# Rotation and norm of queries and keys in a dilated attention: from GpSimd and VectorE to VectorE alone

## The chip, the cores and the metric

One NeuronCore of a Trainium2 chip runs the whole program. The metric is the device time of one execution in microseconds (us). Before the change the median of three runs is 1305.77 us (1304.62 to 1307.18).

## The reference, cut to what matters

A decoder trunk of two layers works on one sequence of 256 tokens with 1024 channels in float32. Each layer is SwiGLU, attention, SwiGLU. The attention of layer 0 is a mixture of three dilations; the change is in how its queries and keys are made.

```python
def dilated_mixer(u, w_qkv, q_gain, k_gain, w_o):
    qkv = (u @ w_qkv).reshape(b, s, N_DIL, 3, N_HEADS, HEAD_DIM)      # 3 dilations, q k v, 16 heads of 64
    for g in range(N_DIL):
        q = rope(rms_norm(qkv[:, :, g, 0], q_gain[g]))
        k = rope(rms_norm(qkv[:, :, g, 1], k_gain[g]))
        o, lse = dilated_attention(q, k, qkv[:, :, g, 2], DIL_WINDOWS[g], DIL_RATES[g])
...
    w = jax.nn.softmax(jnp.stack(lses, axis=0), axis=0)               # merge of the dilations
```

The attention of layer 1 (`nsa_mixer`) is sparse: compressed blocks, selected blocks and a window, with two shared key heads. The change touches the order in which its units may end.

## The kernel before, in words

Every product is made of three matmuls on a high and a low part of each operand. A weight block arrives by DMA as 128x2048 float32 in a ring of four (`st`). Each half of it (128x1024) is cast on ScalarE to the high part (`wh`, line 387) and subtracted on VectorE to the low part (`wl`, line 413); both rings hold six halves. Between the weights stand blocks of `w_ada`, which VectorE reduces (line 393). All blocks come in one fixed order.

The dilated attention works through four head groups of four heads. For each of them `dilated` (line 1062) makes three projections of queries and keys, one for each dilation (`project`, 48 matmuls of 512 columns on lines 849 to 851, with four halves of weights), then two projections of values. A projection uses its first two halves in matmuls 1 to 24 and its last two in 25 to 48. Each projection of queries and keys is followed by a task, `qk_task` (line 919). There are twelve of these tasks. One task does, for both tiles of 128 tokens: squares on ScalarE (860); rotation, which is three multiplications on VectorE (890, 894) and an addition (895); sums of squares (864); an inverse root by a seed (877, 879) and three Newton steps (`newton`, lines 577 to 590); a multiplication of the rotated values with the result (938); and eight transposes on TensorE (906), whose copies go to ScalarE (912). Before the change the additions, the Newton steps and the last multiplications are on GpSimd, for VectorE the Newton step has three instructions instead of four.

Then come the units (`dil_unit`), four in a head group: scores on TensorE (967, 969), mask and maximum on VectorE (975), exponentials on ScalarE (983), division on VectorE (989, 991), transposes (906), copies on ScalarE and VectorE (914), and the product with the values (1007), which after the second unit of a head pair is split into two parts (275, 276).

The order of the instructions on each engine is fixed when the program is built, and each engine works through its queue in that order. A planner, `_Clock`, decides it with a model of each engine's time: a task says with `clk.V(n)`, `clk.G(n)` and `clk.on(...)` how long its parts take, and yields the time at which its next part is to be issued; `fill` issues weight splits and `w_ada` reductions while the modelled VectorE is not too far ahead. So a number in `qk_task` sets behind how many matmuls the task's transposes stand in TensorE's queue, and which splits stand ahead of a task and which behind it in VectorE's.

In the sparse attention a unit (`nsa_unit`, line 1436) is one head pair and one tile of queries. Two units share one half of a PSUM bank (`opair`), and before the change the unit of the second tile copies it out.

Of the kernel before, what the change touches and what calls it, by code (L numbers as in the profile page):

```python
# [72 lines left out]
TT = 2  # L73
# [150 lines left out]
class _Kernel:  # L224
# [194 lines left out]
    def fill(self):  # L419

        clk = self.clk
        while not self.hold:
            T = clk.now + self.slack
            if self.lows and self.lows[0][0][2] < clk.now + self.lag and clk.free["V"] < T:
                self.low()
# [6 lines left out]
            e = self.queue[self.qpos][0]  # L432
            if self.staged[self.qpos][1] > T:
                return
            if e[0] == "w":
                if len(self.halves) >= self.released + self.depth or clk.free["A"] > T:
                    return
            elif clk.free["V"] > T:
                return
# [134 lines left out]
                if len(self.halves) < self.released + self.depth and self.queue[self.qpos][0][0] == "w":  # L574
                    self.emit()

    def newton(self, eng, x, y, n):

        nc = self.nc
        t = self.small(n, f"rs_t{n}")  # L580
        eng.tensor_tensor(out=t, in0=y, in1=y, op=ALU.mult)  # L581
        z = self.small(n, f"rs_y{n}")
        if eng is nc.gpsimd:
            eng.tensor_tensor(out=t, in0=t, in1=x, op=ALU.mult)  # L584
            eng.tensor_scalar(out=t, in0=t, scalar1=-0.5, scalar2=1.5, op0=ALU.mult, op1=ALU.add)  # L585
            eng.tensor_tensor(out=z, in0=t, in1=y, op=ALU.mult)  # L586
        else:
            eng.scalar_tensor_tensor(out=t, in0=t, scalar=-0.5, in1=x, op0=ALU.mult, op1=ALU.mult)
            eng.scalar_tensor_tensor(out=z, in0=t, scalar=1.5, in1=y, op0=ALU.add, op1=ALU.mult)
        return z  # L590
# [8 lines left out]
    def modulated(self, gs, sh, timed=False):  # L599
# [22 lines left out]
        self.hold = False  # L622
        T = self.clk.on("V", 800 * KC, self.clk.now)
        self.clk.free["A"] = max(self.clk.free["A"], T)
# [243 lines left out]
        return self.head_newton(x, self.head_seed(x, n), n, eng)  # L868

    def head_newton(self, x, y, n, eng=None):  # L870
        for _ in range(3):
            y = self.newton(eng or self.nc.gpsimd, x, y, n)
        return y

    def head_seed(self, x, n):
# [43 lines left out]
    def qk_task(self, ps, q, k, g):  # L919

        nc = self.nc
        x = self.small(16, "qkx")
        R = []
        clk = self.clk
        sq = [self.head_squares(ps[tt], 8) for tt in range(TT)]
        for tt in range(TT):
            clk.A(512, clk.now)
            T = clk.G(512, clk.V(1280, clk.now))
            R.append(self.rope(ps[tt].rearrange("p (a r d) -> p a r d", r=4, d=HD),
                               self.dtab[g][:, 0, tt], self.dtab[g][:, 1, tt]).rearrange("p a r d -> p (a r) d"))  # L930
        for tt in range(TT):
            self.head_sums(x[:, tt * 8:(tt + 1) * 8], sq[tt])
            T = clk.V(512)
        rs = self.head_rstd(x, 16)
        T = clk.on("G", 1700, clk.on("V", 400, T))
        for tt in range(TT):
            T = clk.G(512)
            nc.gpsimd.tensor_tensor(out=R[tt], in0=R[tt],  # L938
                                    in1=rs[:, tt * 8:(tt + 1) * 8].unsqueeze(2).to_broadcast([P, 8, HD]),
                                    op=ALU.mult)  # L940
        yield T
        for tt in range(TT):
            c = slice(tt * P, (tt + 1) * P)
            self.transpose4((q[:, :, c], k[:, :, c]), R[tt].rearrange("p h d -> p (h d)"))
# [491 lines left out]
    def nsa_unit(self, kv, pr, qt, oh, ol):  # L1436
        nc, clk = self.nc, self.clk
# [3 lines left out]
        n = (qt + 1) * P  # L1441
# [50 lines left out]
        half = len(pts) // 2  # L1492
        o = self.opair(pr)
        steps = [(b, tt) for b in range(2) for tt in range(qt + 1)]
        while not self.done[kv]:
            yield clk.now + 500.0
        yield "P", 265.0 * (len(steps) + 1), {}, {"u": 1}
        for e in range(2):
            r = slice(e * 64, e * 64 + 64)
            mm(out=o[r, qc], lhsT=self.vpr[kv][:, pr, r], rhs=self.pcT[kv][:, qc], start=True, stop=False)  # L1500
        for i, (b, tt) in enumerate(steps):
            for e in range(2):
                vc = (b * 2 + kv) * HD
                mm(out=o[e * 64:e * 64 + 64, qc], lhsT=self.vkv[:, tt, vc:vc + HD], rhs=pts[e * half + i],
                   start=False, stop=i == len(steps) - 1)
        if qt == 1:
            yield "A", 270.0
            j = kv * 4 + pr
            nc.scalar.copy(out=oh[j], in_=o)
            yield "V", 340.0  # L1510
            nc.vector.tensor_tensor(out=ol[j], in0=o, in1=oh[j].bitcast(F32), op=ALU.subtract)
            self.odone.add(j)

    def nsa_mixer(self, u, gate_fn, prep):
        clk = self.clk
# [1 line left out]
        halves = self.filler  # L1517
        self.warm(AF.Exp)
        self.slack = SL
        self.nsa = {}  # L1520

        self.normed, self.ready, self.done = [False, False], [0, 0], [False, False]
        self.taken, self.blocks = [False, False], False
# [31 lines left out]
        p = self.tmp((P, 2, S))  # L1555
# [304 lines left out]
```

## Time and profile before

| | before |
|---|---|
| median of three runs | 1305.77 us |
| profiled execution, its own time | 1304.5 us |
| its span | 1302.7 us |
| TensorE busy | 1224.2 us, 94% |
| VectorE busy | 976.3 us, 75% |
| GpSimd busy | 255.3 us, 20% |

The span runs from the first to the last instruction; 1.8 us of the profiled execution lie outside it. The dilated attention fills 232 to 560 us of the span. A busy share is a mean over stages; what an engine waited for is read in its own stage.

### The profile page before, as it was taken

To read this page: it belongs to the slowest core of one execution; us is meant where nothing else is said; L and a number is where in the kernel's file an instruction comes from. 1 tells how busy PE (TensorE), PEld (TensorE's weight loads), DVE (VectorE), ACT (ScalarE), POOL (GpSimd) and SP (SyncE) were. 2 spreads that over 40 slices of the span, in tenths; PEclk is the share of its full clock that TensorE was granted. 3 is DMA by queue.
4 is the path that set the end of the run, shared out by engine and by line. 5 is a ranking of instruction groups with operands and counts; after the bars stand their busy time and mean duration, and the time that the engine had idled before them with its cause. 6 is when DMAs were issued, how large, how long until landed. Compare 5 with 4: busy or idle time off the path is not lost.

```text
span 1302.7 us, 23375 instructions
## 1 busy us (share of the span) xinstructions
PE 1224.2 (94%) x9373; PEld 1146.2 (88%) x9373; DVE 976.3 (75%) x1743; ACT 646.3 (50%) x1126; POOL 255.3 (20%) x356
## 2 busy tenths in 40 slices
PE   4899999789989898899999999999999889999998
PEld 3899999677777687799999999989998778999998
DVE  6788886866768677578888878878778997766652
ACT  4545554434445444456545446545435477654441
POOL 3460010462433525110000100030001353000000
PEclk9999999989999999899999999999999899999999
DMA  8889877534353544245888956776983003466650
GB/s 324 303 300 341 325 302 280 196 148 173 133 203 148 197 134 163 91 163 206 327 321 320 343 208 242 272 276 244 334 311 142 33 2 132 162 257 227 239 198 17
DMA packets 42733, 284.50 MB, mean 218 GB/s; under 512 B 5249, under 2 KB 6273, under 8 KB 9346
## 3 DMA queue, kind: packets, MB, share of 16 engines
q1 hardware_dynamic: 42626, 283.02, 58.8%
q8 instruction: 73, 1.20, 0.4%
q14 instruction: 34, 0.28, 0.1%
HBM read 281.96 MB, written 1.05 MB: 217 GB/s over the span
## 4 chain that ended last, share of the span: by engine, by line
PE 73%; DVE 13%; POOL 8%; ACT 3%; issue 2%; DMA 0%; SPq 0%; ACTq 0%; DVEq 0%; POOLq 0%
PE mm L466 18%; PE mm L467 18%; PE mm L468 18%; PE mm L849 3%; PE mm L850 3%; PE mm L851 3%; DVE wl L413 2%; PE tp L906 2%; POOL y L938 2%; POOL rs_t L581 2%; POOL rs_t L584 2%; POOL rs_y L586 2%; POOL rs_t L585 1%; DVE y L1455 1%; DVE st L393 1%
## 5 line engine op out<-in xcount | busy, mean ns | idle before, releaser
L413 DVE TENSOR_TENSOR wl<-st,wh 128x1024 fp32r<-128x1024 f32 x361 | 436.3, 1234 | 94.4 <-ACT wh L387 94.0
L387 ACT CAST wh<-st 128x1024 fp32r<-128x1024 f32 x361 | 369.4, 1048 | 137.3 <-PE mm L468 45.3
L466 PE MATMUL mm<-uh,wh 128*128 128x256 f32 x1304 | 366.5, 281 | 1.6 <-DVE y L738 1.6
L467 PE MATMUL mm<-uh,wl 128*128 128x256 f32 x1304 | 367.9, 282 | 0.0
L468 PE MATMUL mm<-ul,wh 128*128 128x256 f32 x1304 | 365.0, 280 | 0.0
L468 PEld LDWEIGHTS mm<-ul,wh 128*128 128x128 f32 x1304 | 246.8, 189 | 0.0
L466 PEld LDWEIGHTS mm<-uh,wh 128*128 128x128 f32 x1304 | 244.5, 187 | 1.9 <-DVE y L738 1.8
L467 PEld LDWEIGHTS mm<-uh,wl 128*128 128x128 f32 x1304 | 245.0, 188 | 0.0
L466 PE MATMUL mm<-y,wh 128*128 128x256 f32 x832 | 233.4, 281 | 0.1
L467 PE MATMUL mm<-y,wl 128*128 128x256 f32 x832 | 232.4, 279 | 0.0
L468 PE MATMUL mm<-y,wh 128*128 128x256 f32 x832 | 232.2, 279 | 0.0
L393 DVE CUSTOM_DVE_ANT_0 st<-st,cact 128x1024 f32<-128x1024 f32 x152 | 186.7, 1258 | 0.0
L466 PEld LDWEIGHTS mm<-y,wh 128*128 128x128 f32 x832 | 156.4, 188 | 1.1 <-issue 0.9
L467 PEld LDWEIGHTS mm<-y,wl 128*128 128x128 f32 x832 | 156.4, 188 | 0.0
L468 PEld LDWEIGHTS mm<-y,wh 128*128 128x128 f32 x832 | 156.4, 188 | 0.0
L849 PE MATMUL mm<-wh,uh 128*128 128x512 f32 (+1 forms) x336 | 135.0, 402 | 0.0
L850 PE MATMUL mm<-wl,uh 128*128 128x512 f32 (+1 forms) x336 | 131.0, 390 | 0.1
L851 PE MATMUL mm<-wh,ul 128*128 128x512 f32 (+1 forms) x336 | 130.3, 388 | 0.0
L524 POOL TENSOR_TENSOR y<-y 128x256 f32<-128x256 f32 x20 | 22.8, 1138 | 360.3 <-ACT y L505 360.3
L895 POOL TENSOR_TENSOR y<-y 128x512 f32<-128x512 f32 (+1 forms) x26 | 32.3, 1251 | 265.4 <-DVE y L894 157.5
L737 ACT ACTIVATE y<-mm 128x256 f32<-128x256 f32 x84 | 32.2, 383 | 94.2 <-PE mm L468 94.0
L849 PEld LDWEIGHTS mm<-wh,uh 128*128 128x128 f32 x336 | 66.3, 197 | 14.1 <-issue 1.2
(254 smaller groups left out, 1659.2 us busy)
## 6 DMA issues: line engine op xcount, KB each, us to landing
st<-w_in SPq DMA_DIRECT2D x88, 1024.0 KB, 5.1
st<-w_ada SPq DMA_DIRECT2D x76, 1024.0 KB, 5.7
st<-w_out SPq DMA_DIRECT2D x44, 1024.0 KB, 6.8
st<-w_qk SPq DMA_DIRECT2D x24, 1024.0 KB, 4.8
st<-w_va SPq DMA_DIRECT2D x8, 1024.0 KB, 4.7
st<-w_o SPq DMA_DIRECT2D x8, 1024.0 KB, 4.8
st<-w_vb SPq DMA_DIRECT2D x4, 1024.0 KB, 5.0
st<-w_q SPq DMA_DIRECT2D x4, 1024.0 KB, 6.8
```

What stands on the lines that cost most here:

```text
L387: nc.scalar.copy(out=wh, in_=src)
L393: nc.vector.tensor_tensor_reduce(out=src, in0=src, in1=self.cact, scale=1.0, scalar=0.0, op0=ALU.mult, op1=ALU.add, accum_out=self.mod[:, ...
L413: (self.nc.gpsimd if eng == "G" else self.nc.vector).tensor_tensor(out=o, in0=src[:, c], in1=i.bitcast(F32), op=ALU.subtract)
L466: mm(out=out, lhsT=ah, rhs=bh, start=start, stop=False, **kw)
L467: mm(out=out, lhsT=al, rhs=bh, start=False, stop=False, **kw)
L468: mm(out=out, lhsT=ah, rhs=bl, start=False, stop=stop, **kw)
L581: eng.tensor_tensor(out=t, in0=y, in1=y, op=ALU.mult)
L737: nc.scalar.activation(out=sg, in_=ps[:, 0:S], func=AF.Silu)
L849: mm(out=ps[tt], lhsT=uh[k][:, c], rhs=wh[:, o], start=k == 0, stop=False)
L850: mm(out=ps[tt], lhsT=uh[k][:, c], rhs=wl[:, o], start=False, stop=False)
L851: mm(out=ps[tt], lhsT=ul[k][:, c], rhs=wh[:, o], start=False, stop=k == KC - 1)
L895: (eng or nc.gpsimd).tensor_tensor(out=A, in0=A, in1=B, op=ALU.add)
```

## The change

The addition of the rotation, the Newton steps and the last multiplication of `qk_task` go to VectorE, and so do their modelled times. The last Newton step of a task writes a tile with a ring of its own (`rs16`). In the sparse attention the unit that ends second, whichever it is, copies the pair out, and a unit waits until the pair before it in the same half bank has been copied.

```diff
     def head_newton(self, x, y, n, eng=None):
-        for _ in range(3):
-            y = self.newton(eng or self.nc.gpsimd, x, y, n)
+        for i in range(3):
+            y = self.newton(eng or self.nc.gpsimd, x, y, n, "rs16" if n == 16 and i == 2 else None)
...
         for tt in range(TT):
             clk.A(512, clk.now)
-            T = clk.G(512, clk.V(1280, clk.now))
             R.append(self.rope(ps[tt].rearrange("p (a r d) -> p a r d", r=4, d=HD),
-                               self.dtab[g][:, 0, tt], self.dtab[g][:, 1, tt]).rearrange("p a r d -> p (a r) d"))
+                               self.dtab[g][:, 0, tt], self.dtab[g][:, 1, tt], nc.vector)
+                     .rearrange("p a r d -> p (a r) d"))
+            T = clk.V(1880, clk.now)
...
-        rs = self.head_rstd(x, 16)
-        T = clk.on("G", 1700, clk.on("V", 400, T))
+        rs = self.head_rstd(x, 16, nc.vector)
+        T = clk.on("V", 2300, T)
         for tt in range(TT):
-            T = clk.G(512)
-            nc.gpsimd.tensor_tensor(out=R[tt], in0=R[tt],
+            T = clk.V(512)
+            nc.vector.tensor_tensor(out=R[tt], in0=R[tt],
...
-        while not self.done[kv]:
-            yield clk.now + 500.0
+        j = kv * 4 + pr
+        while not self.done[kv] or j > 1 and j - 2 not in self.odone:
+            yield clk.now + 300.0
...
-        if qt == 1:
+        self.half_done[j] = self.half_done.get(j, 0) + 1
+        if self.half_done[j] == TT:
             yield "A", 270.0
-            j = kv * 4 + pr
             nc.scalar.copy(out=oh[j], in_=o)
```

VectorE's queue, first head group, before: from the seed of the first task to the start of the second (`wl<-st,wh` is a weight split, `mod<-` a reduction of `w_ada`, `y<-mm` the rotation).

```order
L879 TENSOR_SCALAR rs_y_2859<-qkx 128x16
L413 TENSOR_TENSOR wl<-st,wh 128x1024 x4
L393 ISA st,mod<-st,cact 128x1024
L393 ISA mod 128x1
L393 ISA st,mod<-st,cact 128x1024
L393 ISA mod 128x1
L413 TENSOR_TENSOR wl<-st,wh 128x1024 x2
L890 TENSOR_TENSOR y<-mm,shareA 128x512
```

The same place after, from the first Newton step's end to the splits.

```order
L589 SCALAR_TENSOR_TENSOR rs_y_2863<-rs_t_2861,rs_y_2859 128x16
L581 TENSOR_TENSOR rs_t_2866<-rs_y_2863 128x16
L588 SCALAR_TENSOR_TENSOR rs_t_2866<-rs_t_2866,qkx 128x16
L589 SCALAR_TENSOR_TENSOR rs_y_2868<-rs_t_2866,rs_y_2863 128x16
L581 TENSOR_TENSOR rs_t_2871<-rs_y_2868 128x16
L588 SCALAR_TENSOR_TENSOR rs_t_2871<-rs_t_2871,qkx 128x16
L589 SCALAR_TENSOR_TENSOR rs_2873<-rs_t_2871,rs_y_2868 128x16
L939 TENSOR_TENSOR y<-y,rs_2873 128x512 x2
L413 TENSOR_TENSOR wl<-st,wh 128x1024 x3
```

Nine Newton instructions and two multiplications now stand between a task's seed and the next split; before, the split came next. The first split behind the task is in both the third half of the second projection.

VectorE's queue, first head group, before: from the end of the second task to the start of the third (`y<-mm,shareC`).

```order
L879 TENSOR_SCALAR rs_y_2997<-qkx 128x16
L413 TENSOR_TENSOR wl<-st,wh 128x1024 x2
L393 ISA st,mod<-st,cact 128x1024
L393 ISA mod 128x1
L393 ISA st,mod<-st,cact 128x1024
L393 ISA mod 128x1
L413 TENSOR_TENSOR wl<-st,wh 128x1024 x2
L890 TENSOR_TENSOR y<-mm,shareC 128x512
```

The same place after.

```order
L939 TENSOR_TENSOR y<-y,rs_3008 128x512 x2
L413 TENSOR_TENSOR wl<-st,wh 128x1024 x2
L393 ISA st,mod<-st,cact 128x1024
L393 ISA mod 128x1
L890 TENSOR_TENSOR y<-mm,shareC 128x512
```

Before, all four halves of the projection that runs beside the third task (the values) were split ahead of it. Now two are, and the third and fourth come behind the whole third task.

VectorE's queue, second head group, after: from the end of the fifth task (`rs_3559`) on, with a unit's split, a unit's division and the next unit's mask ahead of the next weight splits.

```order
L939 TENSOR_TENSOR y<-y,rs_3559 128x512 x2
L276 TENSOR_TENSOR y<-o,y 128x256
L990 RECIPROCAL rd<-den 128x2
L992 TENSOR_SCALAR y<-y,rd 128x512 x2
L976 ISA y,mx<-sc,shareB 128x512
L976 ISA mx 128x1
L976 ISA y,mx<-sc,shareB 128x512
L976 ISA mx 128x1
L981 TENSOR_SCALAR nb<-mx 128x2
L413 TENSOR_TENSOR wl<-st,wh 128x1024 x2
```

The same place before, behind the fifth task's seed.

```order
L879 TENSOR_SCALAR rs_y_3621<-qkx 128x16
L989 RECIPROCAL rd<-den 128x2
L991 TENSOR_SCALAR y<-y,rd 128x512 x2
L413 TENSOR_TENSOR wl<-st,wh 128x1024
L914 COPY y<-tp 128x512
L413 TENSOR_TENSOR wl<-st,wh 128x1024
```

Here too the third half of a projection (the third one of the head group) now stands behind a whole task, and behind a unit's work as well. On GpSimd all 192 instructions of the twelve tasks are gone; VectorE has 156 more.

## Rows read from the trace of the kernel before

**Rows 1.** The page's first part: busy time, share of the span and number of instructions of each engine.

```profile
PE 1224.2 (94%) x9373; PEld 1146.2 (88%) x9373; DVE 976.3 (75%) x1743; ACT 646.3 (50%) x1126; POOL 255.3 (20%) x356
```

**Rows 2.** Busy time in stretches of the span: from the start to the end, length, busy us of PE, PEld, DVE, ACT, POOL (with instructions), granted clock of TensorE (1.00 is 2.4 GHz, 0.50 is 1.2 GHz), share of the DMA engines, GB/s. The dilated attention, the end of the SwiGLU stage before it, and the SwiGLU stage after it.

```profile
220.00:240.00 20.00, 20.00 (x140) 18.50 (x139) 15.33 (x35) 9.78 (x19) 0.00 (x0) 1.00 0.31 110
240.00:560.00 320.00, 283.27 (x1601) 229.48 (x1600) 219.60 (x397) 141.42 (x256) 134.98 (x192) 0.94 0.44 163
...
600.00:820.00 220.00, 220.00 (x1862) 219.93 (x1862) 183.77 (x280) 115.08 (x170) 6.13 (x5) 1.00 0.78 288
```

**Rows 3.** The longest wait of TensorE in the whole span: who waited for whom, us in total, times, longest.

```profile
PE tp L906 <- POOL y L938: 34.6, 14, 7.6
```

**Rows 4.** The dilated attention in order of time, at its first task: start us, us, engine, line, operation, and in brackets the idle time before and what ended it.

```profile
244.08 0.40 PE L849 MATMUL mm<-wh,uh 128*128 128x512 f32 x1
244.31 0.40 PE L850 MATMUL mm<-wl,uh 128*128 128x512 f32 x1
...
244.61 0.69 DVE L890 TENSOR_TENSOR y<-mm,shareA 128x512 f32<-128x512 f32 x1 [1.67 <-ACT y L860]
...
245.88 0.68 DVE L890 TENSOR_TENSOR y<-mm,shareA 128x512 f32<-128x512 f32 x1
...
248.74 0.18 DVE L879 TENSOR_SCALAR rs_y<-qkx 128x16 int32<-128x16 int32 x1
248.82 4.66 DVE L413 TENSOR_TENSOR wl<-st,wh 128x1024 fp32r<-128x1024 f32 x4
...
250.10 0.19 PEld L850 LDWEIGHTS mm<-wl,uh 128*128 128x128 f32 x1 [0.48 <-DVE wl L413]
...
250.19 1.08 POOL L584 TENSOR_TENSOR rs_t<-rs_t,qkx 128x16 f32<-128x16 f32 x1
...
258.53 0.22 POOL L584 TENSOR_TENSOR rs_t<-rs_t,qkx 128x16 f32<-128x16 f32 x1
...
260.53 1.69 PE L906 MATMUL tp<-ident,y 128*128 128x128 f32 x6 [7.60 <-POOL y L938]
```

**Rows 5.** Stretches of 10 us around pauses of TensorE, columns as in rows 2.

```profile
250.00:260.00 10.00, 2.88 (x12) 1.99 (x11) 8.08 (x10) 0.90 (x1) 9.02 (x13) 0.75 0.78 302
260.00:270.00 10.00, 9.47 (x36) 7.67 (x37) 4.01 (x9) 4.28 (x8) 3.95 (x4) 0.74 0.31 117
...
440.00:450.00 10.00, 6.36 (x30) 4.88 (x29) 5.08 (x7) 1.74 (x4) 8.15 (x13) 0.97 0.81 312
450.00:460.00 10.00, 10.00 (x67) 9.10 (x66) 4.12 (x4) 5.48 (x11) 0.00 (x0) 0.85 0.31 107
```

**Rows 6.** In order of time, VectorE in the sparse attention: a whole rotation on VectorE, the sums, two multiplications by the inverse root, and small instructions each of which needs the one before.

```profile
1027.11 1.27 DVE L864 TENSOR_REDUCE qkx<-y 128x8 f32<-128x512 f32 x2
1028.41 0.18 DVE L877 TENSOR_SCALAR qkx<-qkx 128x16 f32<-128x16 f32 x1
1028.62 0.17 DVE L879 TENSOR_SCALAR rs_y<-qkx 128x16 int32<-128x16 int32 x1
1028.70 0.68 DVE L890 TENSOR_TENSOR y<-mm,qtab 128x512 f32<-128x512 f32 x1
...
1030.74 0.68 DVE L890 TENSOR_TENSOR y<-mm,qtab 128x512 f32<-128x512 f32 x1
...
1033.21 0.69 DVE L1329 TENSOR_TENSOR y<-mm,rs_y 128x512 f32<-128x512 f32 x1 [0.40 <-POOL rs_y L586]
1033.82 0.68 DVE L1360 COPY y<-tp 128x512 f32<-128x512 f32 x1
...
1041.99 0.25 DVE L1424 RECIPROCAL cden<-cden 128x16 f32<-128x16 f32 x1
1042.28 0.17 DVE L1426 TENSOR_TENSOR cden<-cden,gts 128x16 f32<-128x16 f32 x1
```

**Rows 7.** In order of time, VectorE's Newton step of the row norm before the stage.

```profile
228.35 0.16 DVE L581 TENSOR_TENSOR rs_t<-rs_y 128x2 f32<-128x2 f32 x1
228.55 0.16 DVE L588 SCALAR_TENSOR_TENSOR rs_t<-rs_t,rs_x 128x2 f32<-128x2 f32 x1
228.74 0.16 DVE L589 SCALAR_TENSOR_TENSOR rs_y<-rs_t,rs_y 128x2 f32<-128x2 f32 x1
```

**Rows 8.** The same columns for the four stretches of the stage: from the first projection's start to the mask of the first unit of the first head group (line 975), from there to the first mask of the second head group's units, to that of the third's, and from there to the split after the last unit (line 276). The units of a head group run beside the projections of the next one.

```profile
232.40:303.29 70.89, 56.48 (x236) 43.90 (x235) 46.34 (x79) 29.47 (x49) 38.87 (x48) 0.88 0.51 193
303.29:381.97 78.68, 71.73 (x410) 58.43 (x409) 55.52 (x100) 36.56 (x65) 32.21 (x48) 0.96 0.44 159
381.97:459.47 77.50, 70.32 (x410) 57.33 (x409) 57.26 (x103) 35.50 (x64) 31.69 (x48) 0.98 0.48 179
459.47:560.26 100.79, 92.61 (x588) 76.26 (x587) 68.07 (x136) 44.86 (x88) 32.21 (x48) 0.95 0.35 127
```

**Rows 9.** Groups of instructions by line, from 225 to 570 us: count, busy us, mean ns of one, idle time of the engine before them and what ended it.

```profile
L413 DVE TENSOR_TENSOR wl<-st,wh 128x1024 fp32r<-128x1024 f32 x76 | 92.6, 1248 | 21.3 <-ACT wh L387 21.3
...
L938 POOL TENSOR_TENSOR y<-y,rs_y 128x512 f32<-128x512 f32 x24 | 31.1, 1315 | 0.9
```

**Rows 10.** The same columns as in rows 2 for the part of the sparse attention in which its units run.

```profile
1010.00:1090.00 80.00, 69.57 (x572) 58.65 (x571) 69.56 (x273) 52.18 (x180) 30.91 (x44) 0.91 0.06 19
```

More of the change, by code (lines that the diff above doesn't have):

```diff
@@ L575, in spare, with newton @@
                     self.emit()
-    def newton(self, eng, x, y, n):
+    def newton(self, eng, x, y, n, name=None):
         nc = self.nc
@@ L581, in newton @@
         eng.tensor_tensor(out=t, in0=y, in1=y, op=ALU.mult)
-        z = self.small(n, f"rs_y{n}")
+        z = self.small(n, name or f"rs_y{n}")
         if eng is nc.gpsimd:
@@ L1519, in nsa_mixer @@
         self.slack = SL
-        self.nsa = {}
+        self.nsa, self.half_done = {}, {}
         self.normed, self.ready, self.done = [False, False], [0, 0], [False, False]
```

## The prediction

> **What bounds the kernel now.** I read the page's busy shares first. TensorE is busy for 94% of the span [rows 1], so nearly every gain has to come out of its pauses or its clock. The windows by stage say where those are: in the SwiGLU stage TensorE is busy for all of 220 us at a clock of 1.00, in the dilated attention for 283.3 of 320 us at 0.94 [rows 2]. So 320 - 283.3 = 36.7 us of pauses lie in the stage that the change touches. A clock of 0.94 is some 0.06 x 320 x 2 = 38 us at 1.2 GHz; work done at that level takes twice as long, so half of them is lost, less what falls into pauses (5.5 us of the first one, [rows 5]): I put the clock's cost at 16 us. The list of waits names the cause: the task's transposes waited 34.6 us for the multiplication on GpSimd, in 14 pauses [rows 3].
>
> The first task shows the mechanism in order of time [rows 4]. VectorE ends the seed at 248.92, then starts four weight splits, and while these run a GpSimd instruction on 128x16 elements takes 1.08 us; later, at 258.53, the same instruction takes 0.22 us. With twelve of them and four wide ones behind each other, the transposes stand ready in TensorE's queue for 7.6 us. The next stretch of 10 us has a granted clock of 0.74, about 5 us at 1.2 GHz; after a pause of 3.6 us the next stretch has 0.85, that is 0.15 x 10 x 2 = 3 us at 1.2 GHz, a loss of half of it [rows 5]. So a long pause costs itself and some 1.7 to 2.4 us behind it.
>
> The Trainium skill ("SBUF — State Buffer", Who interferes with whom) says that a VectorE instruction with two SBUF inputs and a GpSimd instruction that reads SBUF exclude each other, the later one waiting for the whole of the other. The 1.08 against 0.22 us agree, since a split is such an instruction. By that rule VectorE gains as well where GpSimd falls silent: a split takes 1248 ns on the mean in this stage [rows 9] and 4.66 / 4 = 1.17 us or less in a row [rows 4], so at most 0.08 x 76 = 6 us of VectorE's time.
>
> **The change, part by part.**
>
> *What goes.* All 192 GpSimd instructions of the twelve tasks, and with them the 34.6 us [rows 3].
>
> *What VectorE takes on.* Today a task's rotation costs it 245.88 - 244.61 = 1.27 us a tile of tokens [rows 4]; a rotation wholly on VectorE takes 1030.74 - 1028.70 = 2.04 us [rows 6]. Two tiles are 4.1. Sums: 1028.41 - 1027.11 = 1.3. Two small instructions: 0.4. Nine Newton instructions, each needing the one before: 0.20 us from start to start at 128x2 [rows 7], 0.29 behind a reciprocal at 128x16 [rows 6]. The trace has no Newton step on 128x16 on VectorE, so the nine cost 1.8 to 2.6 us; I take 1.8, since these are no reciprocals. Two multiplications at 1033.82 - 1033.21 = 0.61 from start to start [rows 6], 1.25 with the wait ahead; the upper bound is GpSimd's 1315 ns each [rows 9]. A task is then 4.1 + 1.3 + 0.4 + 1.8 + 1.25 = 8.85 us in one piece on VectorE, at most 11, where it was 4.1. Twelve times 4.7 is 56 us on an engine that is busy for 219.6 of the stage's 320 [rows 2]: 276 us. TensorE's work without pauses and at full clock is 283 - 16 = 267. VectorE becomes the longer of the two here, and its queue has one order, so what counts is what stands behind those 8.85 us.
>
> *What stands behind them.* I step through the new order in the four stretches of [rows 8], with a split at 1.15 us, a reduction of `w_ada` at the same, 0.232 us for a matmul of 512 columns (244.31 - 244.08, [rows 4]) and 0.9 us for eight transposes.
>
> First stretch. Task 1 begins at 244.6 as before and ends at 253.45; the third half of the second projection is split behind it, ready at 254.65. TensorE reaches its matmul 26 at 244.0 + 25 x 0.232 = 249.8: a pause of 4.9 us where there were 7.6 (before, this split came first and cost 0.48, [rows 4]). VectorE goes on with six splits and two reductions (9.2 us) and task 2 (262.6 to 271.5), three more (275.0), task 3 (to 283.85), a reduction, and the third half of the values, ready at 286.15. TensorE comes to that half at 279.1: a pause of 7.1 us. With 0.7 us for small ones, 12.7. The stage's work up to the first scores is 195 matmuls and 28 transposes, 48.3 us from 232.4, so they begin at 232.4 + 48.3 + 12.7 + 2.2 for the clock behind the long pause = 295.6, and the first mask at 296.5. Before, it was at 303.3 [rows 8]: minus 6.8 us.
>
> Second stretch. Two pauses. From the end of its second projection TensorE needs 8.6 us to the third half of the third one (three matmuls, a product, scores, 22 matmuls); VectorE needs 0.7 for the squares, 8.85 for task 5, 0.4 + 1.1 + 1.5 for a unit's split, division and the next mask, and 1.15 for the split, 13.7 in all: 5.1 us. Then task 6's transposes stand 27 matmuls (6.3 us) behind their projection, and the task is ready after 1.0 + 8.85: 3.6 us. With 0.3 for a small one and 1.7 of clock twice that is 12.4. Before, the stretch had 78.7 - 71.7 = 7.0 us of pauses, and 0.04 x 78.7 = 3.2 for the clock (twice that time at 1.2 GHz, half of it lost) [rows 8]: plus 2.2 us.
>
> Third stretch. The queue has the same shape, 12.1 us; before, 77.5 - 70.3 = 7.2 of pauses and 0.02 x 77.5 = 1.6 of clock [rows 8]: plus 3.3.
>
> Fourth stretch, to the last split. Task 11's transposes stand only three matmuls and eight transposes behind their projection: 9.75 - 2.3 = 7.5 us of pause, 1.8 of small ones, 2.4 of clock, 11.7. Task 12's now stand behind 90 matmuls and wait for nothing. Before, 100.8 - 92.6 = 8.2 of pauses and 0.05 x 100.8 = 5.0 of clock [rows 8]: minus 1.5.
>
> *Sum.* -6.8 + 2.2 + 3.3 - 1.5 = -2.8 us. So the pauses for GpSimd (34.6) come back as pauses for VectorE of nearly the same length, in fewer and longer pieces.
>
> *The rest.* The model's times order instructions but cost nothing themselves. The new ring `rs16` adds no instruction. In the sparse attention the planner, at another point of its clock, lets units end in another order, with one unit's scaling more on GpSimd and five instructions fewer on VectorE; TensorE pauses there for 80 - 69.6 = 10.4 us [rows 10]; nothing in the rows says which way a new order shifts them, so I bound it by a third of them, 3.5 us to either side, and take 0. The added condition is the planner's own and no instruction waits on the chip for it. Past the reorderings the queues are the same, so what the stage gains, the end gains.
>
> The profiled execution takes 1304.5 us, 1.8 more than its span and 1.3 less than the median of the runs shown. 1304.5 - 2.8 = 1301.7; on the median's footing 1303.0. I say 1303.
>
> **The rivals.**
>
> *VectorE keeps up, and the pauses go.* If TensorE reaches the splits and transposes later than I step it, the clock stays at 2.4 GHz, since no pause is then long. Without the clock's share (2.2 + 3.4 + 3.4 + 2.4 = 11.4) my sum is -14.2, or 1291 to 1292. For it: the tasks' times that the planner now uses (2 x 2.0 + 1.2 + 2.3 + 1.2 = 8.8 by its own formulas) are those of the rows, where before it gave GpSimd 1700 ns for three Newton steps, of which two alone took 258.53 - 250.19 = 8.3 us [rows 4]. Against it: the splits behind tasks 1, 3 and 5 in the new order.
>
> *VectorE becomes the bound, slower.* The place is the same third half behind a task, and its price is the task's length. I have stepped about seven pauses. Each us that a task takes over 8.85 comes back in nearly all of them, once or, where two tasks lie ahead, twice: some 8 us. At the Newton bound of 2.6 (+0.8) this is +6.5, and with multiplications as dear as GpSimd's (+1.4) another +11. From 0.35 us a task on, the change loses. A value between, with +1.4 us a task, gives +11.2 - 2.8 = +8.4 us, or 1314. For it: VectorE would have 276 us of work in a stage of some 317, 87%, with ScalarE's copies waiting in order as well. Against it: the rotation's, the sums' and the Newton step's times are all read on VectorE itself.
>
> The Trainium skill ("Perfetto Trace Analysis", Optimizing Scalar/DVE Operations) gives the rule behind this rival: with VectorE saturated, moving work from it to GpSimd may pay; the change goes the other way. VectorE at 219.6 of 320 us was not saturated, and at 276 it nearly is.
>
> *That the change doesn't do what it says* is excluded by the order: the 192 instructions are gone from GpSimd's queue.
>
> **How the numbers follow.** The likeliest case, pauses exchanged, has 0.50 and 1298 to 1308 as its own range. VectorE keeping up has 0.22 (1284 to 1298), VectorE as the bound 0.28 (1308 to 1320). A measurement of this kernel can't tell less than 0.2%, 2.6 us, from no change: faster is below 1303.2, slower above 1308.4. Of the likeliest case half lies below 1303.2 and half within; of the slower one 0.01 lies within. Faster 0.25 + 0.22 = 0.47, same 0.25 + 0.01 = 0.26, slower 0.27. The range reaches to both rivals' middles and leaves about a tenth out on each side: 1288 to 1315.
>
> **What would show it.** GpSimd has no instruction of the tasks; the first multiplication starts 7.6 us behind the task's first rotation instruction on VectorE. TensorE's waits for line 938 are gone, and in their place stand waits for line 413 and for the new multiplication (line 939) on VectorE, 30 us or more together, the longest at about 279 to 286 us of the span. The first mask comes near 296.5, and the next two stretches each take 2 to 3 us longer than before. The granted clock of the stage is still below 0.97. If TensorE's pauses in the stage are under 20 us, or its clock is 1.00 throughout, the steps through the order are wrong and the kernel is faster than I say; if they are over 45 us, a task takes longer than 8.85.

## The result and the profile after

The changed kernel is slower: 1318.5 us median (1317.99 to 1319.42) against 1305.8 us for the kernel before on the same chip, a ratio of 1.0094, 95% interval [1.008, 1.0108]. The prediction was 1303, in a range of 1288 to 1315.

The profile of the kernel after: first its busy shares, then the chain of work that ended last, by engine:

```profile
PE 1227.4 (93%) x9373; PEld 1148.0 (87%) x9373; DVE 1018.6 (77%) x1894; ACT 644.0 (49%) x1127; POOL 123.4 (9%) x166
```

```profile
PE 72%; DVE 19%; ACT 4%; issue 2%; POOL 1%; DMA 1%; SPq 0%; ACTq 0%; DVEq 0%; POOLq 0%
```

The task's work has left GpSimd (255.3 us of the whole span in [rows 1], 123.4 here). VectorE's share of the final chain is now 19%, where it was 13%. What TensorE waited for, over the whole span (total, times, longest):

```profile
PE mm L850 <- DVE wl L413: 21.1, 7, 6.0
PE tp L906 <- DVE y L939: 9.6, 2, 6.7
...
PE mm L849 <- ACT wh L387: 6.7, 1, 6.7
PE mm L467 <- DVE wl L413: 4.0, 3, 2.4
PE tp L906 <- ACT y L912: 3.6, 3, 1.7
```

The 34.6 us of [rows 3] are gone. In their place stand waits for weight splits (413), for the new multiplication (939), and, on the third row, one that no step of the prediction has: a wait for a cast on ScalarE (line 467 is a matmul with split weights as well, in part behind the stage). Stretches of the stage, with the columns of [rows 2]; the last four lines end at the first masks and the last split, as in [rows 8]:

```profile
240.00:560.00 320.00, 276.45 (x1507) 222.37 (x1505) 257.17 (x543) 132.61 (x244) 0.00 (x0) 0.93 0.43 158
232.40:298.66 66.26, 55.59 (x241) 44.81 (x240) 57.14 (x117) 29.25 (x50) 0.00 (x0) 0.90 0.46 168
298.66:382.39 83.73, 71.66 (x410) 57.03 (x409) 68.92 (x141) 36.03 (x66) 0.00 (x0) 0.96 0.46 166
382.39:467.27 84.88, 74.60 (x410) 59.97 (x409) 66.73 (x140) 35.06 (x64) 0.00 (x0) 0.92 0.45 165
467.27:569.87 102.60, 90.84 (x579) 74.52 (x578) 78.27 (x175) 45.06 (x88) 0.00 (x0) 0.95 0.34 122
```

The first mask comes 4.6 us earlier than before (298.66 against 303.29), and then each stretch is longer than its counterpart: 83.73 against 78.68, 84.88 against 77.50, 102.60 against 100.79. The stage ends 9.6 us late, and the span is 13.6 us longer.

One task on VectorE, in order of time, is what the prediction said:

```profile
245.41 0.69 DVE L890 TENSOR_TENSOR y<-mm,shareA 128x512 f32<-128x512 f32 x1 [1.67 <-ACT y L860]
...
251.11 0.18 DVE L581 TENSOR_TENSOR rs_t<-rs_y 128x16 f32<-128x16 f32 x1
251.32 0.17 DVE L588 SCALAR_TENSOR_TENSOR rs_t<-rs_t,qkx 128x16 f32<-128x16 f32 x1
...
253.00 1.29 DVE L939 TENSOR_TENSOR y<-y,rs 128x512 f32<-128x512 f32 x2
254.21 1.22 DVE L413 TENSOR_TENSOR wl<-st,wh 128x1024 fp32r<-128x1024 f32 x1
```

253.00 - 245.41 = 7.6 us to the multiplication, 8.80 us to the next split, and 0.21 us from one Newton instruction to the next.

The wait for the cast shows a chain through three engines. Behind the fifth task, in order of time, on VectorE, ScalarE and TensorE:

```profile
339.34 1.29 DVE L939 TENSOR_TENSOR y<-y,rs 128x512 f32<-128x512 f32 x2
...
341.87 0.68 DVE L976 CUSTOM_DVE_ANT_0 y<-sc,shareB 128x512 f32<-128x512 f32 x1
...
343.21 0.17 DVE L981 TENSOR_SCALAR nb<-mx 128x2 f32<-128x2 f32 x1
...
343.41 0.72 ACT L984 ACTIVATE y<-y,nb 128x512 f32<-128x512 f32 x1 [10.49 <-DVE nb L981]
...
344.84 1.97 ACT L387 CAST wh<-st 128x1024 fp32r<-128x1024 f32 x2
...
345.92 0.79 PE L849 MATMUL mm<-wh,uh 128*128 128x512 f32 x1 [6.73 <-ACT wh L387]
```

A unit's mask stands behind the whole task on VectorE. ScalarE's exponentials need that mask, so ScalarE, whose queue has one order, sat idle for 10.49 us; and the casts of the next weights stand behind the exponentials in that queue. TensorE waited 6.73 us for such a cast, though the cast itself needs nothing from the task. ScalarE's waits for line 981 (980 in the kernel before) went from 48.3 to 70.8 us between 240 and 560 us:

```profile
ACT y L984 <- DVE nb L981: 70.8, 15, 10.5
```

### The profile page after: what moved, and what is told of

Same layout as the page of the kernel before. It is cut to its first block, busy times and chain, and to the rows that moved or that the text cites. A ratio compares the mean times of both kernels' runs of the same rounds, so it can differ in the third digit from the quotient of the medians.

```text
span 1316.3 us, 23266 instructions
## 1 busy us (share of the span) xinstructions
PE 1227.4 (93%) x9373; PEld 1148.0 (87%) x9373; DVE 1018.6 (77%) x1894; ACT 644.0 (49%) x1127; POOL 123.4 (9%) x166
## 4 chain that ended last, share of the span: by engine, by line
PE 72%; DVE 19%; ACT 4%; issue 2%; POOL 1%; DMA 1%; SPq 0%; ACTq 0%; DVEq 0%; POOLq 0%
PE mm L467 17%; PE mm L466 17%; PE mm L468 17%; DVE wl L413 4%; PE mm L850 4%; PE mm L849 4%; PE mm L851 3%; PE tp L906 2%; DVE st L393 2%; DVE y L1456 1%; ACT wh L387 1%; DVE y L894 1%; DVE y L895 1%; DVE qkx L864 1%; PE sc L466 1%
## 5 line engine op out<-in xcount | busy, mean ns | idle before, releaser
L850 PE MATMUL mm<-wl,uh 128*128 128x512 f32 (+1 forms) x336 | 131.2, 391 | 21.1 <-DVE wl L413 21.1
L850 PEld LDWEIGHTS mm<-wl,uh 128*128 128x128 f32 x336 | 64.9, 193 | 35.4 <-DVE wl L413 24.9
L849 PEld LDWEIGHTS mm<-wh,uh 128*128 128x128 f32 x336 | 64.5, 192 | 21.2 <-ACT wh L387 7.2
```

The lines of the kernel that those rows point to most:

```text
L849: mm(out=ps[tt], lhsT=uh[k][:, c], rhs=wh[:, o], start=k == 0, stop=False)
L850: mm(out=ps[tt], lhsT=uh[k][:, c], rhs=wl[:, o], start=False, stop=False)
```

## The experiments

The change does two things to the dilated attention: it moves work to VectorE, and it changes the numbers by which the planner orders every queue. The first experiments take these apart. "Old order" is the one that the planner makes from the task's old numbers, "new order" that from the new ones. The theories were:

1. The order: splits and units now stand behind one piece of 8.8 us.
2. The work: VectorE has some 56 us more to do, and that costs in whatever order.
3. The waits for GpSimd in the kernel before were themselves a matter of order.

**The sparse attention's edits alone.**

```diff
-        while not self.done[kv]:
-            yield clk.now + 500.0
+        j = kv * 4 + pr
+        while not self.done[kv] or j > 1 and j - 2 not in self.odone:
+            yield clk.now + 300.0
```

(and the copy by whichever unit ends second)

> The kernel before with the two edits in the sparse attention alone (units may end in either order); the rotation and norm stay as they were. The prediction took these edits at 0 and bounded them by 3.5 us to either side. By the theory that the whole loss comes out of the dilated attention (theories 1 and 2 alike): 1304 to 1308 us against 1305.8. By the rival that the new order of the sparse units costs what is missing (the stage itself ended 9.6 us later, the time is 12.7 us longer): 1308 to 1309 us.

Measured: 1306.8 us, ratio 1.0007 [0.9998, 1.0016]. These edits cost nothing that can be told from no change; the loss is made by the dilated attention.

**Work and order apart.** Work on VectorE in the old order is the changed kernel with the planner's old numbers:

```diff
-            T = clk.V(1880, clk.now)
+            T = clk.G(512, clk.V(1280, clk.now))
...
-        T = clk.on("V", 2300, T)
+        T = clk.on("G", 1700, clk.on("V", 400, T))
...
-            T = clk.V(512)
+            T = clk.G(512)
             nc.vector.tensor_tensor(out=R[tt], in0=R[tt],
```

> The changed kernel, with the planner's times for the task as they were before: the work runs on VectorE, TensorE's order is the one from before. Theory 1 (the new order is the loss: the planner now sets the splits and the units behind the 8.8 us piece): the loss goes with the order, 1306 us or less. Theory 2 (VectorE's own 56 us more, wherever they stand): 1315 to 1322 us, as with the changed kernel or worse, since TensorE now also meets the transposes earlier than they are ready.

Work on GpSimd in the new order is the opposite: the kernel before with the sparse edits and the new numbers.

> The kernel before (work on GpSimd, Newton steps and wide ones), with the sparse edits and with the planner's times of the changed kernel: TensorE's order is the new one. Theory 1 (the order is the loss): about 1318 us or more. Theory 2 (VectorE's work is the loss): about 1306 us. Theory 3 (the 34.6 us for GpSimd were a matter of an order that expected the task after 1.7 us of Newton steps; the new order leaves the transposes more time): below 1300 us.

Measured, with the kernel before at 1306.9 (the changed kernel: at 1305.8):

| | old order | new order |
|---|---|---|
| work on GpSimd | 1306.8 | 1321.6, ratio 1.011 [1.0097, 1.0124] |
| work on VectorE | 1284.7 (1281.9 to 1287.8), ratio 0.983 [0.9808, 0.9852] | 1318.5, ratio 1.0094 [1.008, 1.0108] |

In the old order the move of the work gains 22 us. The new order loses 34 us with the work on VectorE and 15 us with it on GpSimd. The traces show that each column is one order on TensorE: the transposes of the first three tasks stand behind 84, 141 and 189 matmuls of projections in both kernels of the old order, behind 75, 141 and 171 in both of the new one, and TensorE's later order agrees in the same way. Theory 2 falls, and theory 3 in this form too: the waits for GpSimd stayed (37.6 us, against 34.6), and the new numbers don't even put the transposes later there. The kernel with the work on VectorE in the old order once more, under another label and on another chip:

> A second look at v_work_old_order, beside the run above on the same chip: 1282 to 1288 us if the order stays as good there, so that the 34 us between the orders stand.

It took 1282.9 us in one run. The profile of the first one (of its run of 1287.8 us): the stage to its own last split, then the same of the changed kernel.

```profile
232.40:542.80 310.40, 286.64 (x1640) 234.01 (x1639) 272.44 (x572) 144.62 (x267) 0.00 (x0) 0.96 0.47 170
```

```profile
232.40:569.87 337.47, 292.69 (x1634) 236.33 (x1633) 271.05 (x572) 145.40 (x267) 0.00 (x0) 0.93 0.42 153
```

TensorE's waits in the first of the two:

```profile
PE tp L906 <- DVE y L992: 9.4, 4, 3.1
PE o L1008 <- DVE y L914: 6.3, 3, 2.3
PE mm L850 <- DVE wl L413: 4.6, 1, 4.6
PE mm L849 <- DVE y L894: 2.2, 1, 2.2
```

(A window of fixed length, 240 to 560 us, would mislead here: in a faster kernel it takes in part of the next stage, in which TensorE hardly pauses.) VectorE does the same work in both stages, 272 and 271 us, once in 310 us (88%) and once in 337 (80%). TensorE's pauses are 23.8 us against 44.8. Only one wait for a split is left on line 850 where the changed kernel had seven. So a busier VectorE goes with the shorter stage, and its total doesn't explain the loss; what stood in which place does.

**What the order does to the splits.** Between the seventh task and the eighth, VectorE's queue in the old order has four splits and two reductions of `w_ada`. In order of time, up to the eighth task's first rotation (other rows left out):

```profile
394.84 1.22 DVE L413 TENSOR_TENSOR wl<-st,wh 128x1024 fp32r<-128x1024 f32 x1
...
400.32 1.22 DVE L413 TENSOR_TENSOR wl<-st,wh 128x1024 fp32r<-128x1024 f32 x1
401.45 1.22 DVE L393 CUSTOM_DVE_ANT_0 st<-st,cact 128x1024 f32<-128x1024 f32 x1
...
403.20 1.21 DVE L413 TENSOR_TENSOR wl<-st,wh 128x1024 fp32r<-128x1024 f32 x1
...
405.75 1.22 DVE L413 TENSOR_TENSOR wl<-st,wh 128x1024 fp32r<-128x1024 f32 x1
406.89 1.22 DVE L393 CUSTOM_DVE_ANT_0 st<-st,cact 128x1024 f32<-128x1024 f32 x1
...
408.04 0.68 DVE L890 TENSOR_TENSOR y<-mm,shareA 128x512 f32<-128x512 f32 x1
```

The changed kernel has two splits and no reduction between the same tasks:

```profile
407.99 1.22 DVE L413 TENSOR_TENSOR wl<-st,wh 128x1024 fp32r<-128x1024 f32 x1
411.45 0.69 DVE L914 COPY y<-tp 128x512 f32<-128x512 f32 x1 [2.24 <-PE tp L906]
412.06 1.22 DVE L413 TENSOR_TENSOR wl<-st,wh 128x1024 fp32r<-128x1024 f32 x1
413.19 0.68 DVE L890 TENSOR_TENSOR y<-mm,shareA 128x512 f32<-128x512 f32 x1
```

So in the changed kernel the next halves come behind the whole eighth task, and TensorE waits for the first of them:

```profile
426.01 0.79 PE L850 MATMUL mm<-wl,uh 128*128 128x512 f32 x1 [3.85 <-DVE wl L413]
```

The code has a rule that does this. `fill` puts a split or a reduction ahead of its need only while the planned time of VectorE lies less than 1500 ns in front of that of TensorE (`slack` is 1500 in this stage, `low` places a split, the last two lines stand ahead of a reduction):

```python
T = clk.now + self.slack
if self.lows and self.lows[0][0][2] < clk.now + self.lag and clk.free["V"] < T:
    self.low()
...
elif clk.free["V"] > T:
    return
```

A task that is charged with 1880 x 1.04 + 70 twice, 512 x 1.04 + 70 four times and 2300 ns puts VectorE's planned time some 8.8 us in front, so for a long while no split is put ahead; each is then placed when its matmul comes, behind whatever was placed before it. The old numbers charge 4.4 us. Two experiments edit this rule alone:

```diff
-            if self.lows and self.lows[0][0][2] < clk.now + self.lag and clk.free["V"] < T:
+            if self.lows and self.lows[0][0][2] < clk.now + self.lag and clk.free["V"] < T + self.vx:
...
-            elif clk.free["V"] > T:
+            elif clk.free["V"] > T + self.vx:
```

with `vx` 4700 in the dilated attention of the changed kernel,

> The changed kernel with one number added to the planner's rule in `fill`: in the dilated attention a split or a reduction is put ahead of its need while VectorE's planned time is less than 1500 + 4700 ns in front of TensorE's (1500 in before and after). 4700 is about what the change adds to a task's charge on VectorE. If the loss is that this rule, with the task charged at 8 us, no longer puts splits ahead of the tasks: the waits for line 413 (21.1 us) mostly go, 1280 to 1300 us. If the loss comes from the other choices of the new order (units, transposes): 1310 us or more.

and -4700 in the kernel with the work on VectorE in the old order.

> The counterpart: v_work_old_order (1284.7 us; task charged as before) with the same number subtracted, 1500 - 4700 ns, so that splits are put ahead only when VectorE's planned time is well behind TensorE's. If the rule on putting splits ahead is the cause: waits for splits come back and the time is 1305 us or more. If it isn't: within 8 us of 1285.

Measured: 1297.0 us, ratio 0.9931 [0.9913, 0.9949], and 1389.5 us, ratio 1.0638 [1.0621, 1.0655]. So editing the rule gives back 21.5 us one way and costs 105 us the other. The second number shows the direction and not the size of what the change did, since 4700 ns are taken off throughout the stage and not only while a task is charged. Nor do the two runs isolate the splits: the planner's later choices follow from what `fill` does. The transposes of the third task, for one, stand behind 191 matmuls in the first of them (171 in the changed kernel, 189 in the old order), and those of the first task behind 54 in the second (84 in the old order). TensorE's waits in the second one (lines of this kernel are one further on, 414 is the split):

```profile
PE mm L851 <- DVE wl L414: 88.2, 20, 8.9
PE mm L850 <- ACT wh L388: 10.6, 6, 2.5
```

Splits are waited for 20 times, and casts with them. In the first one the expectation was met in the time and missed in the mechanism:

```profile
PE mm L851 <- DVE wl L414: 22.4, 4, 6.5
...
PE mm L850 <- DVE y L895: 5.3, 4, 3.1
```

The waits for splits did not go; they became four in place of seven, with nearly the same sum (22.4 against 21.1), while the waits for tasks (9.6) and for the cast (6.7) are gone. Its stage ends at 550.6 us, 19.3 earlier than in the changed kernel, with 32.3 us of TensorE's pauses in place of 44.8 and a clock of 0.95 in place of 0.93. So the rule changes the time by far more than the noise, but not in the way that was expected of it: which of TensorE's waits go with it is another question. Further ahead, with 9000:

> As after_splits_ahead (1297.0 us), with 9000 in place of 4700 ns. Of the 34 us between the two orders with the work on VectorE (1318.5 and 1284.7), after_splits_ahead gave back 21.5. If the rest is the rule on putting splits ahead as well: 1285 to 1291 us. If the rest lies in the other choices that the charge changes (units, transposes): 1294 to 1300 us.

1292.7 us, ratio 0.9891 [0.9874, 0.9907], between the two expectations. Of the 34 us between the orders, 26 come back with an edit of the rule. That the order is the loss is shown; how much of it lies in the places of the splits, and how much in those of units and transposes, which moved along with the rule, no run tells apart.

**One piece or several; transposes later.** Theory 1 had a simpler form: the piece is too long. `pieces` cuts it:

```diff
+        yield "V", 1250.0
         for tt in range(TT):
             self.head_sums(x[:, tt * 8:(tt + 1) * 8], sq[tt])
-            T = clk.V(512)
+        yield "V", 2300.0
         rs = self.head_rstd(x, 16, nc.vector)
-        T = clk.on("V", 2300, T)
+        yield "V", 1250.0
+        T = clk.free["V"] + 120.0
         for tt in range(TT):
-            T = clk.V(512)
```

> The changed kernel with the task cut into four pieces on VectorE (rotations; sums; Newton steps; last multiplications): between them the planner may put weight splits and sparse or dilated units. By theory 1 (the one piece of 8.8 us in front of the splits is the loss): 1285 to 1300 us. If only the place of the transposes counts: the task's end comes still later than in the changed kernel, 1310 us or more unless they are put off as well.

1316.2 us, ratio 1.0066 [1.005, 1.0082]: nothing gained beside the changed kernel's 1.0094. The waits for splits on line 850 are gone, but now TensorE waits eleven times for a task's end:

```profile
PE tp L906 <- DVE y L940: 30.9, 11, 3.6
```

So cutting the piece only traded one wait for another, and the kernel of 1284.7 us has the same piece uncut: that form of the theory falls. And with only the transposes put off, `yield T + 8000.0` in place of `yield T`:

> The changed kernel with one number added: the planner is told that the task's result is there 8000 ns later than VectorE's own time for it; VectorE's clock in the planner stays charged with the task's 8.8 us. If the loss is that the transposes stand too early behind their task: 1290 us or less. If the loss is that the planner, with VectorE charged, puts the splits and units of the stage behind the task: 1305 us or more.

1313.2 us, ratio 1.0047 [1.0032, 1.0062], as the second reading expected: 21.2 us of waits for splits stayed, in three pieces.

**The price of a task's length.**

```diff
-        for i in range(3):
-            y = self.newton(eng or self.nc.gpsimd, x, y, n, "rs16" if n == 16 and i == 2 else None)
+        k = 1 if n == 16 else 3
+        for i in range(k):
+            y = self.newton(eng or self.nc.gpsimd, x, y, n, "rs16" if n == 16 and i == k - 1 else None)
```

> The changed kernel in the same order, with one Newton step in place of three in the dilated attention's norms (the other two are left out), so each of the twelve tasks is 6 x 0.21 = 1.26 us shorter on VectorE. By the prediction's price of 8 us for each us of a task: 1318.5 - 10 = 1308 us. If the pauses come from places where two tasks and units stand ahead (each us paid in about twelve places): 1303 us. If VectorE's work is not what TensorE waits for: 1314 us or more.

1302.3 us, ratio 0.9967 [0.9957, 0.9978]. The function also serves the query norms of the sparse attention, so two Newton steps are left out there as well, on GpSimd; the price is therefore read in the stage. Its last split starts at 556.3 us of the span against 569.9, so 13.6 us go for 1.26 us a task: 10.8 us for each us of a task. That lies between the prediction's 8 and the twelve places of the second reading, whose time (1303) was met.

**Work on GpSimd, and the planner told how long it takes.** Theory 3 in its other form: the kernel before with the sparse edits and

```diff
-            T = clk.G(512, clk.V(1280, clk.now))
+            T = clk.on("G", 1300, clk.V(1280, clk.now))
...
-        T = clk.on("G", 1700, clk.on("V", 400, T))
+        T = clk.on("G", 8000, clk.on("V", 400, T))
...
-            T = clk.G(512)
+            T = clk.on("G", 1300)
```

> The kernel before (work on GpSimd), with the sparse edits, and with the planner told 1300 ns for each wide GpSimd operation and 8000 ns for the Newton steps, about what the trace of before shows, in place of 512 and 1700. TensorE's order then has the transposes later. Theory 3 (the waits for GpSimd come from the planner's too short time): most of the 34.6 us of waits and of the clock's 16 us go, 1275 to 1290 us. By the rival (the transposes put off only put off the scores behind them, and TensorE runs out of other work): 1300 to 1312 us.

1271.8 us, ratio 0.9734 [0.972, 0.9747], the fastest of all and 3 us below the expected range. Its stage to its own last split, and what is left of the waits for GpSimd:

```profile
232.40:527.50 295.10, 281.63 (x1652) 230.33 (x1651) 234.80 (x416) 146.50 (x266) 144.85 (x192) 0.98 0.49 182
```

```profile
PE tp L906 <- POOL y L938: 7.1, 4, 5.6
```

Of 34.6 us of waits for GpSimd 7.1 are left, TensorE pauses for 13.5 us in the stage, the clock is 0.98. The first task's transposes stand 27 matmuls later in TensorE's queue than in the kernel before (111 in place of 84). The same order with the work on VectorE, and the same kernel with 12000 in place of 8000:

> The changed kernel (work on VectorE) in the order of g_work_true_cost: the planner is told the same numbers as there (1300 ns for each wide operation and 8000 ns for the Newton steps on an engine of its own), so TensorE reaches each task's transposes late. If the place of the transposes in TensorE's order is what counts, and either engine is done by then: within 5 us of g_work_true_cost, 1267 to 1277 us. If VectorE's 56 us more still cost something of their own in that order (splits late behind the task): 1280 to 1290 us, as v_work_old_order.

> As g_work_true_cost, with 12000 in place of 8000 ns for the Newton steps. g_work_true_cost still waited 5.6 us once for GpSimd, and the Newton steps took more than 8 us there. If more room only helps: 1262 to 1271 us. If the transposes then hold up the scores behind them: 1274 to 1285 us.

1294.6 us, ratio 0.9903 [0.9885, 0.9922], above both expectations, and 1278.9 us, ratio 0.9789 [0.9773, 0.9806], as the second reading expected. In an order that gives GpSimd its time the move to VectorE costs 22.8 us, as much as it gains in the old order: there TensorE waits for units' divisions (line 992, 9.2 us) and copies (914, 6.9 us) behind tasks. So VectorE's added work does cost in an order that suits GpSimd. Of the two values for the Newton steps 8000 is the better one; no others were run.

## Why the prediction was wrong, step by step

*What goes, and the task's length.* Right: the 34.6 us are gone, the task has 7.6 us to its multiplication and 8.80 in all (predicted 8.85), so Newton steps and multiplications sat at the lower bounds.

*The four stretches.* This is the step that failed. Change of each against before:

| stretch | predicted | measured |
|---|---|---|
| first | -6.8 | -4.6 |
| second | +2.2 | +5.0 |
| third | +3.3 | +7.4 |
| fourth | -1.5 | +1.8 |
| sum | -2.8 | +9.6 |

In the first, the pauses came where they were stepped (4.64 us at the second projection's third half, predicted 4.9; 6.03 at the values', predicted 7.1), and it began 0.8 us late. In the second, third and fourth two terms were too small: the pauses in all three, and the clock's cost in the last two. The second stretch has 83.73 - 71.66 = 12.1 us of pauses where 9.0 were stepped. Its steps went through VectorE's queue and left out ScalarE's, where casts stand behind exponentials that wait for a mask behind a task: at the third half behind the fifth task TensorE waited 6.73 us for the cast and 0.46 for the split, where 5.1 were stepped for the split alone, and 1.66 us more went to a copy on ScalarE. For the third stretch "the queue has the same shape" was assumed and not stepped, and it doesn't hold: the waits there are two for splits, 3.85 us behind the eighth task and the following one behind the ninth, and none for a task's transposes, where 3.6 were stepped:

```profile
450.94 0.79 PE L850 MATMUL mm<-wl,uh 128*128 128x512 f32 x1 [5.22 <-DVE wl L413]
```

That its pauses came out at 84.88 - 74.60 = 10.3 us, near the 8.7 that were carried over, is in part luck. And the clock: 0.92 in the third stretch, which by the prediction's own reckoning is 0.08 x 84.9 = 6.8 us where 3.4 were taken. Together the three stretches have 34.1 us of pauses where 27.0 were stepped, and by that reckoning 15.2 us for the clock where 9.2 were taken.

*The rest.* The sparse edits at 0: right (1.0007). "What the stage gains, the end gains" missed 4.0 us: behind the stage's last split the gate's values (line 489) now stand behind two more weight splits on VectorE, 572.47 - 569.87 = 2.6 us after it where it was 0.4, and smaller differences follow.

*What was to show it.* The waits for lines 413 and 939 are 21.1 + 9.6 + 4.0 = 34.7 us (30 or more were expected), the clock of the stage is 0.93 (below 0.97), TensorE's pauses 320 - 276.45 = 43.6 us. The first mask came at 298.7 us (296.5 expected), and the next two stretches were 5.0 and 7.4 us longer, where 2 to 3 were expected. The signs were there and the account was still 12 us off, since its pauses were 1.6 to 3.1 us too short in each of the last three stretches, and the clock's cost half of what it was in two of them.

*The rivals.* "VectorE becomes the bound, slower" has the right sign, the right place (a third half behind a task) and nearly the right price for a us (10.8 for 8), but its condition, a task longer than 9.2 us, was not met: the task is 8.80 us long. And with 272 us of VectorE's work in a stage of 310 us the kernel was faster than before by 22 us, so that its total isn't the cause. "VectorE keeps up" didn't come about with the new numbers; with the old ones it nearly did (1284.7 us). The Trainium skill ("Perfetto Trace Analysis", Optimizing Scalar/DVE Operations) says that with VectorE saturated a move of work to GpSimd may pay, and adds that it might not, since the two share a port. Here the fastest kernel does keep it on GpSimd, but by the order: with the old numbers the same choice loses 22 us against VectorE.

*The deeper fault.* "The model's times order instructions but cost nothing themselves" was taken as a reason to step the new order as given and to book its pauses on the moved work. The runs show it the other way round: the work alone gains 22 us, and the new numbers lose 34 with the work moved and 15 without. The description of the kernel ahead of the prediction names the rule, that `fill` issues splits only while the modelled VectorE is not too far ahead, and the rows on the change show its effect (two halves split ahead of the third task where there were four), and neither was followed through the later head groups.

## What to carry to other kernels

Where a planner orders the queues, an edit of its costs is an edit of its own: run the work with the old numbers and the numbers with the old work before blaming either. A truer number can make a worse order when other rules, here also how far ahead splits may be put, hang on the same engine's clock; a truer number for GpSimd gave the best kernel of those run. And a queue is stepped through on every engine that a late instruction feeds: a mask that comes late on VectorE delays a cast on ScalarE that needs nothing from it.

## What had not been expected of the hardware

While GpSimd works, a small VectorE instruction can take as long as one of GpSimd's wide ones. In the fastest kernel, VectorE's two small instructions of the second task, and GpSimd's additions of the same time:

```profile
262.42 0.93 DVE L877 TENSOR_SCALAR qkx<-qkx 128x16 f32<-128x16 f32 x1
263.45 1.16 DVE L879 TENSOR_SCALAR rs_y<-qkx 128x16 int32<-128x16 int32 x1
...
262.04 2.55 POOL L895 TENSOR_TENSOR y<-y 128x512 f32<-128x512 f32 x2
```

In the changed kernel, where GpSimd is silent:

```profile
268.77 0.17 DVE L877 TENSOR_SCALAR qkx<-qkx 128x16 f32<-128x16 f32 x1
268.98 0.18 DVE L879 TENSOR_SCALAR rs_y<-qkx 128x16 int32<-128x16 int32 x1
```

An instruction of 0.17 us took 0.93 and 1.16, and each of the two ended about when one of GpSimd's additions (some 1.27 us each) did. This is not the rule: of the 24 such instructions of the twelve tasks six took 0.68 to 1.29 us in the fastest kernel, and in the kernel before, where GpSimd had the same work, none took over 0.28. First one line's, then the other's shortest, median and longest in ns, in the fastest kernel:

```profile
L877 DVE TENSOR_SCALAR qkx<-qkx x12: 224/284/1294, 249.0 to 485.4; 128x16 f32<-128x16 f32 x12
L879 DVE TENSOR_SCALAR rs_y<-qkx x12: 174/175/1161, 249.3 to 486.8; 128x16 int32<-128x16 int32 x12
```

No run isolates this. The mean split took 1226 ns in the changed kernel (225 to 580 us), 1248 ns in that of before [rows 9], and 1285 ns in the fastest kernel (225 to 580 us, with some of the next stage):

```profile
L413 DVE TENSOR_TENSOR wl<-st,wh 128x1024 fp32r<-128x1024 f32 x91 | 113.7, 1285 | 7.6 <-ACT wh L387 7.6
```

The Trainium skill ("SBUF — State Buffer", Who interferes with whom) says that a VectorE instruction with two inputs in SBUF contends with a GpSimd instruction that reads SBUF, and names `tensor_scalar`, which these small instructions are, among those that can enter a mode in which VectorE and GpSimd exclude each other. The splits agree, and so do the six long small ones; the other eighteen show no such wait. Even so the kernel that bears this on both engines was the fastest: TensorE waited 7.1 us for GpSimd in it.
